# Second ConvFFN of a decoder trunk: eight of its eleven pairs of inner tiles by Strassen's seven products, in four groups instead of two

## The chip, the cores and the metric

The kernel runs on one core of a Trainium2 chip. Its time is the device time of one execution in microseconds (us); lower is better. The profile is one execution recorded by the hardware profiler: PE is the matrix engine (TensorE), PEld its loading of stationary operands, DVE is VectorE, ACT is ScalarE, POOL is GpSimd and SP is SyncE, which here only issues transfers.

## The reference

Two layers on one sequence of 512 tokens and width 1024, all in float32: a Conformer convolution module, a ConvFFN, a retention layer, a second ConvFFN, then a last RMSNorm. The change is in the second ConvFFN, whose inner width F is 2816, that is 22 tiles of 128:

```python
def conv_ffn(x, w_in, dw_w, dw_b, w_out):
    h = x @ w_in                          # 512x1024 @ 1024x5632
    a, u = jnp.split(h, 2, axis=-1)
    a = causal_dwconv(a, dw_w, dw_b)      # three taps along the tokens
    return (jax.nn.silu(a) * u) @ w_out   # 512x2816 @ 2816x1024
...
h = rmsnorm(x, norm_ffn_g[i])
x = x + conv_ffn(h, ffn_w_in[i], ffn_dw_w[i], ffn_dw_b[i], ffn_w_out[i])
...
return rmsnorm(x, final_g)
```

## The kernel before

**Precision.** Each float32 operand is held as a high part (a cast to fp32r) and a low part (the difference). One product of tiles takes three matmuls: high with high, low with high, high with low (`mm3`, lines 309 to 311). Every weight chunk is therefore loaded raw (`wr`, four buffers of 128 x 2048, issued on SP), cast by ACT (`wh`, line 239, four buffers of 128 x 1024) and subtracted by DVE (`wl`, line 243, four buffers). `weights()` hands out the current unit of weights and emits the next one.

**Layout.** The residual x is kept transposed: `xT[k]` holds features 128k to 128k+127 on the partitions and the 512 tokens along the free axis.

**The plain form** (`ffn_half`). For each inner tile f, `mm(f)` computes one 128 x 512 tile of `a` (`fa`) and one of `u` (`fu`): 8 tiles of x times 3 matmuls for each, 48 matmuls of 512 columns. A pair of tiles takes two units of weights (four halves of 128 x 1024). x is taken times the norm's gain only; the factor 1/rms (`rb`, made by `n3.stats` and `n3.bcast` in the course of the first tiles) is applied when the tiles are read out. `evac(f)` does that read-out: `ap` = `fa` x `rb` on DVE, three taps (`taps`: ACT, two on DVE, Silu on ACT), `rb` once more on POOL, times `fu` on DVE, and the split into `y_f` high and low. A generator `each` is advanced after every `evac`; a generator `side` is advanced inside it.

**The block form** (`ffn_blocks`, so far used in the first ConvFFN for 14 of its 22 tiles). A pair of inner tiles is a 2 x 2 block product: x cut in two by features (k below 4, k from 4) and in two by tokens (256 columns each), the weights in two by features and into `a` and `u`. Strassen's scheme (Winograd's variant) needs seven block products instead of eight; each is 2 tiles x 4 x 3 = 24 matmuls of 256 columns. The left factors are the four quarters of the normed x and four sums of them (`Factors`: `sums_of(k)` and `normed_split(k)`). The right factors are made from two raw chunks by `pair_factor`: one sum on DVE (`ws`, line 281), and three sums by transfers that add into the raw tile (lines 282, 292 and 294, issued on POOL). The products accumulate in three pairs of PSUM banks, `z`, `x` and `p`; between products ACT copies out `q1`, `u1` and `u2`.

**After a group of tiles** their `y` tiles are taken times the matching rows of `w_out` (`lo`: for the two halves g of the output columns and four tiles tb of tokens, three matmuls of 512 columns for each inner tile), and `finish` adds the result to x. This projection is token major, so x is transposed before it: DVE transposes in blocks of 32 (line 1287) into `xq`, and 16 transfers on SP for each batch (`quarters`, line 433) put the blocks in place in `xt`. Before, that is done by `token_major`, one transpose per inner tile of the first group, in three batches of 3, 3 and 2 tiles of x. In the last projection `finish` also takes the sum of squares, the last norm and the output transfers (lines 1299 to 1313).

**Groups.** `GROUPS` lists for each ConvFFN the ranges of inner tiles and whether each is done in block form. Before, the second ConvFFN has two plain groups, tiles 0 to 11 and 12 to 21.

**Order.** The tile framework orders every engine's instructions at build time by a simulated timeline. It fills an engine's waits with later work that is ready, so the order on an engine differs in places from the order in the code. At run time each engine goes through its list in order.

Of the kernel before, what the change touches and what calls it, by code (L numbers as in the profile page):

```python
# [9 lines left out]
F32 = mybir.dt.float32  # L10
# [6 lines left out]
P = 128  # L17
D = 1024
S = 512
KD = D // P  # L20
NTB = S // P
# [5 lines left out]
NF = F // P  # L27
EPS = 1e-6

GROUPS = [[(0, 8, False), (8, 14, True), (14, 22, True)], [(0, 12, False), (12, 22, False)]]  # L30

# [21 lines left out]
NSH = 9  # L55
GC = P // PH
NM = NSH * PH * GC
XG = ((0, 3), (3, 3), (6, 2))


COLS = {"mg": 16, "fg": 16, "dwb": 8, "lng": 8, "lnb": 8, "taps": CW * KD, "dwp": PH * len(PHASED), "fw0": 4 * NF, "fw1": 4 * NF}
# [95 lines left out]
def trunk(ctx, tc, xt_d, positions, ret_gn_g, final_g, weights_d, cols_d, mats_d, ident_d, decay_d, invf_d, out):  # L157
    nc = tc.nc
    pe, act, dve, pool = nc.tensor, nc.scalar, nc.vector, nc.gpsimd
# [3 lines left out]
    xp = ctx.enter_context(tc.tile_pool(name="xp", bufs=1))  # L163
# [110 lines left out]
    sum_pool = [None]  # L274
# [70 lines left out]
    xT = [xs_all[:, k, :] for k in range(KD)]  # L345
# [8 lines left out]
    class Rstd:  # L354


        def __init__(self, name):
            self.name = name
# [60 lines left out]
    QB = 32  # L419

    def blocks(t):

        return t.rearrange("p (a b q) -> p a b q", a=NTB, q=QB)
# [5 lines left out]
    def quarters(dst, src, *engs):  # L429

        for p in range(P // QB):
            for c in range(P // QB):
                engs[c % len(engs)].dma_start(dst[c * QB:(c + 1) * QB, :, p, :], src[p * QB:(p + 1) * QB, c, :, :])
# [439 lines left out]
    N2 = S // 2  # L873

    class Factors:
        def __init__(self, norm, xs, pool_, other):
            self.norm, self.xs, self.other = norm, xs, other
            self.sums = [pool_.tile([P, 4, 4, N2], F32R, tag=f"s{half}", bufs=1, name=f"{norm.name}s{half}") for half in "hl"]

        def normed(self, k):  # L880
            n = self.norm
            t = xp.tile([P, S], F32, tag="nsq", bufs=2, name=f"{n.name}n{k}")
            dve.scalar_tensor_tensor(out=t, in0=xT[k], scalar=n.gain[:, k:k + 1], in1=n.rb, op0=ALU.mult, op1=ALU.mult)
            return t

# [27 lines left out]
    def ffn_blocks(fp, l, norm, f0, f1, left, side=None):  # L913

        ys = []
        for f in range(f0, f1, 2):
            def bank(which):
                return [psum(f"f{which}{l}_{f + j}")[:, :N2] for j in range(2)]

            def product(pss, which, first=False):  # L920
                w = weights()
                for j, ps in enumerate(pss):
                    for k, (xh, xl) in enumerate(left.factor(which)):
                        mm3(ps, *w(k, j * P, (j + 1) * P), xh, xl, first and k == 0, k == 3, skip_group_check=not first)

            def kept(pss, name):
                tiles = [fp.tile([P, N2], F32, tag=name, bufs=2, name=f"{name}{l}_{f + j}") for j in range(2)]
                for t, ps in zip(tiles, pss):
                    act.copy(t, ps)
                return tiles  # L930

            lo, hi = slice(0, N2), slice(N2, S)
            aps = [fp.tile([P, S + 32], F32, tag="ap", bufs=2, name=f"ap{l}_{f + j}") for j in range(2)]
            us = [fp.tile([P, S], F32, tag="fy", bufs=2, name=f"fy{l}_{f + j}") for j in range(2)]
            z = bank("z")
            product(z, "x11", True)
            q1 = kept(z, "q1")
            x = bank("x")
            product(x, "x12", True)
            for j in range(2):  # L940
                dve.memset(aps[j][:, :2], 0.0)
                dve.tensor_tensor(out=aps[j][:, 2:2 + N2], in0=x[j], in1=q1[j], op=ALU.add)
            p = bank("p")
            product(p, "s1", True)
            product(z, "s2")
            u1 = kept(z, "u1")
            product(z, "s3")
            u2 = kept(z, "u2")
            for j in range(2):
                dve.tensor_tensor(out=us[j][:, hi], in0=p[j], in1=u2[j], op=ALU.subtract)  # L950
            product(z, "x22")
            ts = []
            for j in range(2):
                act.copy(aps[j][:, 2 + N2:2 + S], z[j])
                ts.append(taps(fp, l, f + j, aps[j]))
            product(p, "s4")
            for j in range(2):
                dve.tensor_tensor(out=us[j][:, lo], in0=p[j], in1=u1[j], op=ALU.subtract)
                dve.tensor_tensor(out=us[j], in0=us[j], in1=ts[j], op=ALU.mult)
                ys.append(split(us[j], f"y{l}_{f + j}", ("yh", "yl"), fp))  # L960
                next(side or iter(()), None)
        return ys
# [55 lines left out]
    with ExitStack() as es:  # L1018
        fp = es.enter_context(tc.tile_pool(name="f0", reuse_waits="tile", bufs=8))
        sum_pool[0] = fp  # L1020
        left = Factors(n1, list(n1.xs), fp, lambda name: fp.tile([P, 2, N2], F32, tag="fy", bufs=2, name=name))
# [250 lines left out]


    with ExitStack() as es:
        fp = es.enter_context(tc.tile_pool(name="f1", reuse_waits="tile", bufs=12))
        lp = es.enter_context(tc.tile_pool(name="lp", reuse_waits="tile", bufs=1))
        xt = lp.tile([P, NTB, 4, KD * QB], F32, name="xt")
        fgb = (cos, sin)
        for g in range(2):
            act.dma_start(fgb[g], final_g[512 * g:512 * (g + 1)].partition_broadcast(P))  # L1280

        def token_major():

            for k0, kn in XG:
                xq = lp.tile([P, 4, NTB, kn, QB], F32, tag="xq", bufs=1, name=f"xq{k0}")
                for k in range(kn):
                    dve.transpose(xq[:, :, :, k, :].rearrange("p c t q -> p t c q"), blocks(xT[k0 + k]))
                    yield
                quarters(xt[:, :, :, k0 * QB:(k0 + kn) * QB], xq.rearrange("p c t k q -> p c t (k q)"), nc.sync)

        ssq = sp.tile([P, NTB, 2], F32, tag="ssq", bufs=1, name="ssq")

        def finish(n, g, tb, ps):
            d = xt[:, tb].rearrange("p a (k q) -> p k a q", q=QB)[:, 4 * g:4 * g + 4]
            if n == 0:
                dve.tensor_tensor(out=d, in0=blocks(ps), in1=d, op=ALU.add)
                return
            dv, d = d, xT[2 * tb + g]
            dve.tensor_tensor(out=blocks(d), in0=blocks(ps), in1=dv, op=ALU.add)
            j = xp.tile([P, S], F32, tag="nsq", bufs=2, name=f"junk{tb}{g}")  # L1300
            v = ssq[:, tb, g:g + 1]
            act.activation(j, d, AF.Square, accum_out=v)
            if g == 0:
                dve.tensor_scalar(out=v, in0=v, scalar1=1.0 / D, scalar2=EPS, op0=ALU.mult, op1=ALU.add)
                pool.tensor_tensor(out=d, in0=d, in1=fgb[0], op=ALU.mult)
                return
            vv = sp.tile([P, 1], F32, tag="fv", name=f"fv{tb}")
            dve.tensor_scalar(out=vv, in0=v, scalar1=1.0 / D, scalar2=ssq[:, tb, 0:1], op0=ALU.mult, op1=ALU.add)
            r = rsqrt_small(vv, 1, f"fr{tb}")
            act.activation(xT[2 * tb], xT[2 * tb], AF.Copy, scale=r)  # L1310
            nc.scalar.dma_start(out[0, tb * P:(tb + 1) * P, :512], xT[2 * tb])
            dve.scalar_tensor_tensor(out=d, in0=d, scalar=r, in1=fgb[1], op0=ALU.mult, op1=ALU.mult)
            nc.sync.dma_start(out[0, tb * P:(tb + 1) * P, 512:], d)

        for n, (f0, f1, _) in enumerate(GROUPS[1]):
            ys = ffn_half(fp, 1, n3, f0, f1, () if n else (None, n3.stats, n3.bcast), None if n else token_major())
            nk = len(ys)
            for g in range(2):
                last = n == 1 and g == 1
                ps = [psum(f"lo{n}{g}{tb}") for tb in range(NTB)]  # L1320
                groups = []
                for k0, kn in _out_chunks(f0, f1, last):
                    groups += [(k0 + k, k, w) for w in [weights()] for k in range(kn)]
                    if last and k0 + kn < nk and k0 > 0:
                        continue
                    for tb in range(NTB):
                        for f, k, w in groups:
                            yh, yl = ys[f]
                            mm3(ps[tb], yh[:, tb * P:(tb + 1) * P], yl[:, tb * P:(tb + 1) * P], *w(k, 0, 512),
                                f == 0, f == nk - 1)  # L1330
                        if k0 + kn == nk:
                            finish(n, g, tb, ps[tb])
                    groups = []
# [79 lines left out]
```

## Time and profile before

| | |
|---|---|
| Time before, median of 3 runs | 1281.57 us (1281.56 to 1282.28) |
| Profiled execution, its own time | 1281.37 us |
| Its span, first to last instruction | 1279.6 us |
| Granted TensorE clock | 0.998 |
| Busy: PE, PEld, DVE, ACT, POOL | 1270.1, 1082.6, 882.9, 566.1, 271.0 us |
| HBM read, written | 133.75 MB, 2.10 MB |

The second ConvFFN runs from 911.80 us (first `fa` matmul) to the end of the span. Busy times are sums of instruction times on an engine; matmuls overlap, so the time that one costs in a stream is the distance between starts, which a window's length over its count of matmuls gives (`x` counts also include an instruction that reaches into the window). A line such as `[0.37 <-PE fa L311]` behind an instruction says how long its engine sat idle before it and what ended that.

### The profile page before, as it was taken

The page shows a single profiled execution, that of the slowest core. Times are in us where ns is not written, and L with a number is a line of the kernel's source. Part 1 is how long each engine was busy: PE and PEld are TensorE (multiplying, and loading weights), DVE is VectorE, ACT ScalarE, POOL GpSimd, SP SyncE. Part 2 cuts the span into 40 slices and gives each one's busy share as a digit, 9 for nine tenths or more (in the row PEclk, how much of TensorE's full clock was granted, in tenths as well). Part 3 has the DMA queues.
Part 4 walks back from the last instruction along what each step waited for, and adds up shares of the span by engine and source line. Part 5 has one row for each costly group of instructions (what it writes and reads, how often), then busy time and mean ns, then how long its engine had stood idle before and what let it go on. Part 6 is the DMA issues. An engine that isn't in the chain of part 4 may idle for free.

```text
span 1279.6 us, 16389 instructions
## 1 busy us (share of the span) xinstructions
PE 1270.1 (99%) x6459; PEld 1082.6 (85%) x6459; DVE 882.9 (69%) x1210; ACT 566.1 (44%) x796; POOL 271.0 (21%) x250
## 2 busy tenths in 40 slices
PE   9999999999999999999999999999999999999997
PEld 7889988888998998888888888878888888888886
DVE  6998658884796897589696686695675642355542
ACT  6546644442652665335344345254443431143332
POOL 0957321110100110222212303203311100011111
PEclk9999999999999999999999999999999999999999
DMA  9533331333755663322405315323124432223111
GB/s 331 229 124 107 126 114 66 127 111 83 190 153 133 184 167 130 115 99 81 126 25 187 109 41 173 82 100 132 66 99 123 124 116 99 99 70 128 34 66 66
DMA packets 38957, 151.58 MB, mean 118 GB/s; under 512 B 11232, under 2 KB 16096, under 8 KB 24800
## 3 DMA queue, kind: packets, MB, share of 16 engines
q1 hardware_dynamic: 32256, 134.02, 30.5%
q0 software_dynamic: 3024, 11.01, 4.7%
q10 hardware_dynamic: 3600, 5.52, 1.5%
q8 instruction: 50, 0.82, 0.3%
q14 instruction: 27, 0.22, 0.1%
HBM read 133.75 MB, written 2.10 MB: 106 GB/s over the span
## 4 chain that ended last, share of the span: by engine, by line
PE 97%; DVE 2%; issue 1%; POOL 0%; ACT 0%; POOLq 0%
PE fu L310 4%; PE fa L310 4%; PE fa L311 4%; PE fu L311 4%; PE fa L309 4%; PE fu L309 4%; PE fo L310 3%; PE fo L309 3%; PE fo L311 3%; PE lo L310 3%; PE lo L311 3%; PE lo L309 3%; PE cph L622 3%; PE qk L309 2%; PE qk L310 2%; PE qk L311 2%
## 5 line engine op out<-in xcount | busy, mean ns | idle before, releaser
L243 DVE TENSOR_TENSOR wl<-wr,wh 128x1024 fp32r<-128x1024 f32 (+2 forms) x256 | 314.9, 1234 | 164.4 <-ACT wh L239 161.8
L239 ACT CAST wh<-wr 128x1024 fp32r<-128x1024 f32 (+2 forms) x258 | 264.9, 1030 | 329.2 <-PE lo L310 63.5
L1107 POOL TENSOR_TENSOR gg<-gg,gn 128x512 f32<-128x512 f32 x16 | 27.5, 1721 | 179.3 <-ACT gg L1106 179.3
L998 POOL MEMSET ap<- 128x2 f32 x30 | 2.8, 98 | 277.8 <-DVE ft L972 239.9
L671 DVE SCALAR_TENSOR_TENSOR tp<-hp,prm,tp 128x512 f32<-128x512 f32 x80 | 55.8, 748 | 0.4
L970 ACT ACTIVATE ft<-ap,prm 128x512 f32<-128x512 f32 x44 | 35.9, 815 | 43.2 <-DVE ap L999 42.7
L662 POOL TENSOR_TENSOR pla<-pla,plt 128x512 f32<-128x512 f32 x36 | 49.1, 1366 | 9.7 <-ACT pla L658 5.6
L1003 DVE TENSOR_TENSOR fy<-fu,ft 128x512 f32<-128x512 f32 x30 | 20.6, 688 | 39.3 <-PE fu L311 23.9
L973 ACT ACTIVATE ft<-ft 128x512 f32<-128x512 f32 x44 | 27.7, 632 | 37.2 <-DVE ft L972 36.5
L971 DVE SCALAR_TENSOR_TENSOR ft<-ap,prm,ft 128x512 f32<-128x512 f32 x44 | 33.9, 771 | 11.6 <-ACT ft L970 11.4
L1091 POOL TENSOR_TENSOR rs<-rs 128x512 f32<-128x512 f32 x16 | 24.7, 1559 | 67.4 <-DVE rs L1090 42.3
L1001 POOL TENSOR_TENSOR ft<-ft,n3r 128x512 f32<-128x512 f32 x22 | 32.2, 1464 | 28.7 <-ACT ft L973 28.7
L661 ACT ACTIVATE plt<-hp,prm 128x512 f32<-128x512 f32 x36 | 25.8, 722 | 20.7 <-POOL pla L662 20.2
L972 DVE SCALAR_TENSOR_TENSOR ft<-ap,prm,ft 128x512 f32<-128x512 f32 x44 | 33.9, 771 | 0.8
L467 DVE TENSOR_TENSOR xT<-ro,xT 128x512 f32<-128x512 f32 x32 | 21.6, 682 | 16.5 <-PE ro L311 16.5
L622 PEld LDWEIGHTS cph<-ph,cmat 128*128 128x128 f32 x288 | 32.6, 192 | 0.2
L622 PE MATMUL cph<-ph,cmat 128*128 128x128 f32 x288 | 32.6, 275 | 0.0
L311 PE MATMUL fp<-n1sl,wh 128*128 128x256 f32 x112 | 31.7, 283 | 0.0
L310 PE MATMUL fp<-n1sh,wl 128*128 128x256 f32 x112 | 31.7, 283 | 0.0
L309 PE MATMUL fp<-n1sh,wh 128*128 128x256 f32 x112 | 31.7, 283 | 0.0
L311 PE MATMUL fz<-n1sl,wh 128*128 128x256 f32 x112 | 31.6, 283 | 0.0
L310 PE MATMUL fz<-n1sh,wl 128*128 128x256 f32 x112 | 31.6, 283 | 0.0
(1969 smaller groups left out, 4010.2 us busy)
## 6 DMA issues: line engine op xcount, KB each, us to landing
wr<-in_weights_dram SPq DMA_DIRECT2D x106, 1024.0 KB, 5.0
cmat<-in_mats_dram SPq DMA_DIRECT2D x4, 2304.0 KB, 11.2
wr<-wr POOLq DMA_DIRECT2D x14, 512.0 KB, 4.5
wr<-in_weights_dram POOLq DMA_DIRECT2D x7, 512.0 KB, 5.9
wr<-in_weights_dram SPq DMA_DIRECT2D x4, 512.0 KB, 3.6
wr<-in_weights_dram SPq DMA_DIRECT2D x6, 256.0 KB, 7.7
yt<-yq ACTq DMA_DIRECT2D x24, 64.0 KB, 2.1
yt<-yq SPq DMA_DIRECT2D x24, 64.0 KB, 2.1
```

The source lines that it names most:

```text
L239: latest[0] = act.copy(hi[:, o:o + n], raw[:, s + o:s + o + n])
L243: latest[1] = low_on.get(i, dve).tensor_tensor(out=lo[:, o:o + n], in0=raw[:, s + o:s + o + n], in1=hi[:, o:o + n].bitcast(F32), op=ALU.su ...
L309: pe.matmul(ps, wh, xh, start=first, stop=False, **check)
L310: pe.matmul(ps, wl, xh, start=False, stop=False, **check)
L311: pe.matmul(ps, wh, xl, start=False, stop=last, **check)
L622: pe.matmul(ps[:, g * P:(g + 1) * P], mats[i][g][:, s, :], ph[:, g, NSH - 1 - s:NSH - 1 - s + P], start=s == 0, stop=s == NSH - 1)
L662: gate[0] = pool.tensor_tensor(out=pl, in0=pl, in1=tm, op=ALU.add).ins
L671: dve.scalar_tensor_tensor(out=a, in0=hp[:, t:t + S], scalar=tap(t, i), in1=a, op0=ALU.mult, op1=ALU.add)
L970: act.activation(t, ap[:, 2:2 + S], AF.Identity, scale=wc(2), bias=wc(3))
L971: dve.scalar_tensor_tensor(out=t, in0=ap[:, 1:1 + S], scalar=wc(1), in1=t, op0=ALU.mult, op1=ALU.add)
L972: dve.scalar_tensor_tensor(out=t, in0=ap[:, 0:S], scalar=wc(0), in1=t, op0=ALU.mult, op1=ALU.add)
L1001: scaled = pool.tensor_tensor(out=t, in0=t, in1=norm.rb, op=ALU.mult)
```

## The change

The second ConvFFN gets four groups: tiles 0 to 5 plain, and 6 to 11, 12 to 17 and 18 to 21 in block form, 8 pairs in all. Around it:

- x is transposed at once (8 transposes, then one batch of 16 transfers) in the generator `between`, which runs between the plain tiles; it goes on to make the sums and the quarters for the left factors. The buffer `xq` shares its place (`sh`) with the high parts of the sums.
- `normed(k)` writes x times gain and `rb` in place into `xT[k]`, once, and keeps it.
- `q1`, `u1` and `u2` of the second ConvFFN live in the buffers of the norms (`nacc`, `nsq`).
- `finish` adds to x after each of the first three groups. The last projection has 4 inner tiles, so it has one chunk of weights for each half g.

```diff
-GROUPS = [[(0, 8, False), (8, 14, True), (14, 22, True)], [(0, 12, False), (12, 22, False)]]
+GROUPS = [[(0, 8, False), (8, 14, True), (14, 22, True)], [(0, 6, False), (6, 12, True), (12, 18, True), (18, 22, True)]]
...
-        def __init__(self, norm, xs, pool_, other):
-            self.norm, self.xs, self.other = norm, xs, other
+        def __init__(self, norm, xs, pool_, other, in_place=False):
+            self.norm, self.xs, self.other, self.made = norm, xs, other, {} if in_place else None
...
         def normed(self, k):
             n = self.norm
-            t = xp.tile([P, S], F32, tag="nsq", bufs=2, name=f"{n.name}n{k}")
+            if self.made and k in self.made:
+                return self.made[k]
+            if self.made is None:
+                t = xp.tile([P, S], F32, tag="nsq", bufs=2, name=f"{n.name}n{k}")
+            else:
+                t = self.made[k] = xT[k]
             dve.scalar_tensor_tensor(out=t, in0=xT[k], scalar=n.gain[:, k:k + 1], in1=n.rb, op0=ALU.mult, op1=ALU.mult)
             return t
...
             def kept(pss, name):
-                tiles = [fp.tile([P, N2], F32, tag=name, bufs=2, name=f"{name}{l}_{f + j}") for j in range(2)]
+                if l == 0:
+                    tiles = [fp.tile([P, N2], F32, tag=name, bufs=2, name=f"{name}{l}_{f + j}") for j in range(2)]
+                else:
+                    home, n = ("nacc", 1) if name == "q1" else ("nsq", 2)
+                    t = xp.tile([P, 2, N2], F32, tag=home, bufs=n, name=f"{name}{l}_{f}")
+                    tiles = [t[:, 0], t[:, 1]]
...
-        fp = es.enter_context(tc.tile_pool(name="f1", reuse_waits="tile", bufs=12))
+        fp = es.enter_context(tc.tile_pool(name="f1", reuse_waits="tile", bufs=6))
...
+        sum_pool[0] = fp
...
-        def token_major():
-
-            for k0, kn in XG:
-                xq = lp.tile([P, 4, NTB, kn, QB], F32, tag="xq", bufs=1, name=f"xq{k0}")
-                for k in range(kn):
-                    dve.transpose(xq[:, :, :, k, :].rearrange("p c t q -> p t c q"), blocks(xT[k0 + k]))
+        lefts = []
+
+        def between():
+            xq = fp.tile([P, 4, NTB, KD, QB], F32, tag="sh", bufs=1, name="xq")
+            for k in range(KD):
+                dve.transpose(xq[:, :, :, k, :].rearrange("p c t q -> p t c q"), blocks(xT[k]))
+            yield
+            quarters(xt, xq.rearrange("p c t k q -> p c t (k q)"), nc.sync)
+            left = Factors(n3, list(n3.xs), fp, lambda name: fp.tile([P, 2, N2], F32, tag="fy", bufs=2, name=name), True)
+            lefts.append(left)
+            for k in range(4):
+                left.sums_of(k)
+                if k < 3:
                     yield
-                quarters(xt[:, :, :, k0 * QB:(k0 + kn) * QB], xq.rearrange("p c t k q -> p c t (k q)"), nc.sync)
+            for k in range(KD):
+                left.normed_split(k)
...
-            if n == 0:
+            if n < len(GROUPS[1]) - 1:
                 dve.tensor_tensor(out=d, in0=blocks(ps), in1=d, op=ALU.add)
...
-        for n, (f0, f1, _) in enumerate(GROUPS[1]):
-            ys = ffn_half(fp, 1, n3, f0, f1, () if n else (None, n3.stats, n3.bcast), None if n else token_major())
+        for n, (f0, f1, by_blocks) in enumerate(GROUPS[1]):
+            if by_blocks:
+                ys = ffn_blocks(fp, 1, n3, f0, f1, lefts[0])
+            else:
+                side = between()
+                ys = ffn_half(fp, 1, n3, f0, f1, (None, n3.stats, n3.bcast), each=side)
+                for _ in side:
+                    pass
             nk = len(ys)
             for g in range(2):
-                last = n == 1 and g == 1
+                last = n == len(GROUPS[1]) - 1 and g == 1
```

More of the change, by code (lines that the diff above doesn't have):

```diff
@@ L57 @@
 NM = NSH * PH * GC
-XG = ((0, 3), (3, 3), (6, 2))
 COLS = {"mg": 16, "fg": 16, "dwb": 8, "lng": 8, "lnb": 8, "taps": CW * KD, "dwp": PH * len(PHASED), "fw0": 4 * NF, "fw1": 4 * NF}
```

## The prediction

> **What bounds the kernel now.** I read the page's head, the chain that ended last and the PE's waits first.
>
> ```profile
> span 1279.6 us, 16389 instructions
> ...
> PEclk9999999999999999999999999999999999999999
> ...
> PE 97%; DVE 2%; issue 1%; POOL 0%; ACT 0%; POOLq 0%
> ```
>
> ```profile
> PE warm L179 <- POOL ones L324: 1.0, 1, 1.0
> PE vg3z L311 <- DVE wl L243: 0.5, 1, 0.5
> PE vg3p L311 <- DVE wl L243: 0.5, 1, 0.5
> ```
>
> PE carries 97% of the chain and waits 2.0 us in all, none of it in a ConvFFN; its clock is granted in full throughout. So in the second ConvFFN a microsecond of matmul issue saved is a microsecond of time, as long as every other engine stays ahead. What a matmul costs there, and in the block form, is read from windows: two plain pairs of the second ConvFFN; two block pairs of the first; half of a projection; then the second ConvFFN's first six tiles, the first ConvFFN's plain group, and its last block group.
>
> ```profile
> core 0: us, PE busy (x) PEld busy (x) DVE busy (x) ACT busy (x) POOL busy (x), PEclk, DMA share, GB/s
> 1109.11:1152.63 43.52, 43.52 (x194) 36.05 (x192) 23.80 (x28) 15.85 (x19) 5.31 (x8) 1.00 0.25 85
> 412.84:453.16 40.32, 40.32 (x338) 40.32 (x337) 33.08 (x50) 25.31 (x39) 5.24 (x6) 1.00 0.62 164
> 1043.83:1109.11 65.28, 65.28 (x290) 54.07 (x288) 19.64 (x21) 13.30 (x14) 0.98 (x1) 1.00 0.30 105
> 911.80:977.10 65.30, 65.30 (x289) 53.59 (x288) 42.90 (x51) 27.51 (x36) 11.53 (x13) 1.00 0.28 91
> 190.10:270.40 80.30, 80.30 (x355) 66.12 (x355) 62.86 (x93) 36.69 (x49) 11.30 (x14) 1.00 0.26 89
> 407.10:491.00 83.90, 83.90 (x688) 83.31 (x687) 71.10 (x107) 51.99 (x81) 7.05 (x9) 1.00 0.64 170
> ```
>
> Plain: 2 x 96 = 192 matmuls of 512 columns in 43.52 us, 226.7 ns each, 21.76 us a pair. Block: 2 x 168 = 336 of 256 columns in 40.32 us, 120.0 ns each, 20.16 us a pair. Half the columns cost 53% of the time; in the block window PEld is busy throughout, in the plain one for 83%. So seven eighths of the arithmetic is worth 7.4%, not 12.5%.
>
> **Part by part.**
>
> *The products.* 8 pairs x (21.76 - 20.16) = **-12.80 us** on PE. The projection keeps its 528 matmuls (22 tiles x 24) at 226.7 ns (288 in 65.28 us), whatever the groups: 0.
>
> *The weights.* A plain pair needs four casts and four low parts, a block pair seven of each, one sum on DVE and three adding transfers on POOL.
>
> ```profile
> L243 DVE TENSOR_TENSOR wl<-wr,wh 128x1024 fp32r<-128x1024 f32 (+2 forms) x256 | 314.9, 1234 | 164.4 <-ACT wh L239 161.8
> L239 ACT CAST wh<-wr 128x1024 fp32r<-128x1024 f32 (+2 forms) x258 | 264.9, 1030 | 329.2 <-PE lo L310 63.5
> ...
> wr<-wr POOLq DMA_DIRECT2D x14, 512.0 KB, 4.5
> wr<-in_weights_dram POOLq DMA_DIRECT2D x7, 512.0 KB, 5.9
> ```
>
> Added: ACT 24 x 1.03 = 24.7 us, DVE 24 x 1.23 and 8 sums priced alike = 39.5 us, 24 transfers. All of it lies beside PE: the last block group of the first ConvFFN has DVE busy for 71.10 of 83.90 us (85%) and PE never waits there, with the rotary tables on DVE besides, which the second ConvFFN does not have. Cost 0. If the cover went, PE would pay for the late factor of each product.
>
> *Read-out.* The block form drops POOL's product with `rb` and adds copies of 256 columns on ACT and subtractions on DVE; they are in the windows just used. The four groups add 16 `finish` sums on DVE, about 0.7 us each (11 us over the 260 us or so before the last projection), in the projections, where DVE is busy for 19.64 of 65.28 us: 0.
>
> *Preparation of the left factors.* It must fit beside six plain tiles (65 us) and their projection (6 x 24 x 0.2267 = 32.6 us). DVE was busy for 42.90 of the 65.30 us there. Against the first ConvFFN: that one puts its sums into a plain group of eight tiles, DVE 62.86 of 80.30 us, without a wait of PE. In place, eight of its sixteen `normed` products go; the eight transposes come together.
>
> ```profile
> L1287 DVE STREAM_TRANSPOSE xq<-xT x8: 700/702/712, 947.8 to 1023.7; 128x512 f32<-128x512 f32 x8
> ```
>
> ```profile
> 969.32 10.33 SPq L433 DMA_DIRECT2D xt<-xq  x16
> 979.75 18.04 SPq L212 DMA_DIRECT2D wr<-in_weights_dram  x3
> 1002.66 11.19 SPq L433 DMA_DIRECT2D xt<-xq  x16
> ...
> 1024.42 10.25 SPq L433 DMA_DIRECT2D xt<-xq  x16
> ```
>
> ```profile
> SPq L212 <- DVE wl L243: 789.1, 91, 34.4
> ```
>
> ```profile
> 1015.53 0.71 DVE L1287 STREAM_TRANSPOSE xq<-xT 128x512 f32<-128x512 f32 x1 [2.01 <-DMA xt<-xq]
> ```
>
> Transposes: 8 x 0.70 = 5.6 us of DVE. Transfers: one batch (about 10.3 us of SP's queue) for three (31.8 us), each transfer larger (2 MB / 16 = 128 KB). SP stands idle for a free buffer for 789 us in all, so weight loads behind the batch have room. New is a wait: the sums' first high part on ACT needs the buffer of `xq`, so it waits for the sixteenth transfer. The same kind of wait held DVE for 2.01 us before. Behind it on ACT stand the weight casts, and behind those PE. Their room:
>
> ```profile
> 948.87 1.05 ACT L239 CAST wh<-wr 128x1024 fp32r<-128x1024 f32 x1 [0.37 <-PE fa L311]
> ...
> 949.96 1.23 DVE L243 TENSOR_TENSOR wl<-wr,wh 128x1024 fp32r<-128x1024 f32 x1 [0.73 <-ACT wh L239]
> ...
> 956.79 0.39 PE L309 MATMUL fa<-n3x0h,wh 128*128 128x512 f32 x1
> ```
>
> The low part is done at 951.2 and used from 956.8: 5.6 us. A wait of 2 us disappears in that; one of all 10 us would cost 10.3 - 5.6 = 4.7 us, once. I take 0, since the nearest row is the 2.01; bounds 0 and +4.7. A gain is excluded, as PE has no wait there to lose.
>
> *From the last pair into the last projection.* New: the last group has four tiles, so the projection needs y_20 and y_21 almost at once; before, ten tiles gave cover. Nearest is the first ConvFFN's last pair, whose last product starts its last matmul at 490.83:
>
> ```profile
> 490.83 0.28 PE L311 MATMUL fp<-n1sl,wh 128*128 128x256 f32 x1
> ...
> 495.43 0.68 DVE L386 TENSOR_TENSOR y_20l<-fy,y_20h 128x512 fp32r<-128x512 f32 x1
> 496.04 0.42 DVE L512 TENSOR_SCALAR rot<-rot 128x512 f32<-128x512 f32 x1
> 496.37 0.68 DVE L386 TENSOR_TENSOR y_21l<-fy,y_21h 128x512 fp32r<-128x512 f32 x1
> ```
>
> y_21's low part is there at 497.05, 6.1 us after the product; about 2.2 us of that is rotary work, so 3.9 us here. PE can cover 5.4 us with y_18 and y_19 on all four token tiles (24 matmuls x 0.2267), if the build-time order has not spent them earlier. Bounds: 0, and 6.1 less the 2.5 us before y_21's low part comes up in code order, +3.6. I take **+0.7**, near the lower end, because in the first ConvFFN that order puts projection work (`fo`) ahead of the last pair's product x22 (`fz`), where PE would else have waited:
>
> ```profile
> 481.99 1.09 PE L309 MATMUL fo<-y_14h,wh 128*128 128x512 f32 x4
> 482.92 0.28 PE L309 MATMUL fz<-n1n4h,wh 128*128 128x256 f32 x1
> ```
>
> *The tail.* Each token tile's last `finish` now follows after 12 matmuls (2.72 us) instead of 24 (5.44).
>
> ```profile
> 1272.51 0.69 DVE L1299 TENSOR_TENSOR xT<-lo,xt 128x512 f32<-128x512 f32 x1 [2.34 <-PE lo L311]
> ...
> 1274.28 0.54 POOL L351 TENSOR_TENSOR fr3y<-fv,minus_half 128x1 f32<-128x1 f32 x1 [4.90 <-DVE fv L1308]
> ...
> 1274.85 0.75 DVE L1312 SCALAR_TENSOR_TENSOR xT<-xT,fr3y,sin 128x512 f32<-128x512 f32 x1 [0.66 <-POOL fr3y L351]
> ```
>
> From the sum to the last product on DVE it is 3.09 us, more than 2.72: if the next tile's sum stands behind this tile's last product, each is 0.37 us later than the one before, three times: +1.1. Interleaved it is 0. I take **+0.7**; no gain, since the chain after the last matmul is unchanged.
>
> **Sum:** -12.80 + 0.7 + 0.7 = -11.4 us. The profiled execution took 1281.37 us, 0.2 below the median of 1281.57; from the median the change gives 1270.2, and I say **1270.1 us**.
>
> **The rivals.**
>
> *Preparation crowds PE.* The wait for `xq`'s transfers is longer than ACT's room, or evac of tile 5 stands behind the eight splits and comes late. For it: DVE would be near full there (42.90 + 5.6 + the sums, of 65.30 us). Against it: the first ConvFFN did nearly as much without a wait. Price: up to 4.7 us for the wait and, if y_5 is as late as y_21 can be, up to 3.6 us for that: 2 to 8 us on top, 1272 to 1278.
>
> *A matmul of 256 columns at half the price of one of 512.* Then a block pair would take 168 x 113.3 = 19.04 us, the products would bring 8 x 2.72 = 21.8 us, and the time would be 1261. The block window speaks against it with 120.0 ns over 336 matmuls; only a different stationary operand could change that, and the products are the same. The Trainium skill, "TensorE: Matmul & The Clock Gate", section "Back-to-back issue gap", gives the isolated gap as columns over 2.4 GHz plus 2.5 ns, and adds that with weight loads between them small matmuls fall behind that. By its figures the estimate is 215.8 and 109.2 ns, a saving of 19.0 us over the eight pairs, 1264. The windows, 226.7 and 120.0, decide.
>
> *Slower: the adding transfers come late.* Place: the low half of the weights for the product x22 waits for a transfer that adds into its raw tile.
>
> ```profile
> 474.63 1.05 ACT L239 CAST wh<-wr 128x1024 fp32r<-128x1024 f32 x1 [1.49 <-DMA wr<-wr]
> ...
> 476.33 2.47 DVE L243 TENSOR_TENSOR wl<-wr,wh 128x1024 fp32r<-128x1024 f32 x2
> ```
>
> In the first ConvFFN ACT did wait 1.49 us for one, and DVE had that factor ready at 477.5; the product began only at 482.9, so 5.4 us were left. A transfer that took 4.5 + 5.4 us would begin to hold PE, and every further microsecond costs 8. The sum is used up at 11.4 / 8 = 1.4 us a pair, so it turns slower once landing takes about 11.3 us on every pair, against 4.5 (and 5.9 from HBM). At 2 us a pair: 1286. The load on the queues is that of the first ConvFFN, which speaks against it. The Trainium skill, "SBUF — State Buffer", section "SBUF: two separate sides", warns that a transfer issued from GpSimd can be kept waiting for its descriptors while VectorE runs a two-port operation. No run here shows that by itself; the 4.5 us were measured with DVE busy.
>
> **How the numbers follow.** The forecast, with PE losing under 3 us, 1268.4 to 1272.0: 0.78. Preparation: 0.13. Half price: 0.01. Late transfers: 0.08, of which 0.03 end within 0.2% (2.6 us, about what a measurement of this kernel can tell from no change) of the time before. So faster 0.92, same 0.03, slower 0.05. The range starts at -12.8 (1268.8, less 0.4 for scatter) and reaches 1274.5: all upper bounds of the last two terms (-12.8 + 3.6 + 1.1 = -8.1, 1273.5) and 1 us of preparation.
>
> **What the profile after would show.** Block pairs of 20.16 us in the second ConvFFN, 168 starts 120 ns apart; PE waits still near 2 us in all. ACT idle before the first high part of the sums, released by the transfers of `xq`, under 5.6 us. A PE gap, if any, where the last pair hands over to `lo`, under 1 us. The last four sums on DVE 2.7 to 3.1 us apart. The prediction fails if starts of 256-column matmuls are not 120 ns apart, if PE waits on `wl` in block pairs, or if the plain group of six takes well over 65.3 us.

## The result, and the profile after

| | before | after |
|---|---|---|
| Median of the runs, us | 1281.92 (1281.56 to 1282.29) | 1270.35 (1269.84 to 1270.83) |
| Profiled execution: its own time, us | 1281.37 | 1270.41 |
| Its span, us | 1279.6 | 1268.6 |
| Instructions | 16389 | 17818 |

The ratio is 0.9911, 95% interval 0.9899 to 0.9923. The change makes the kernel faster by 11.6 us (medians); the two profiled executions differ by 11.0 us. The forecast was 1270.1 us.

The page's head after, its clock row and the chain that ended last:

```profile
span 1268.6 us, 17818 instructions
...
PEclk9999999999999999999999999999999999999999
...
PE 95%; DVE 3%; issue 1%; POOL 1%; DMA 0%; ACT 0%; SPq 0%; POOLq 0%; DVEq 0%
```

PE still sets the time, at full clock. DVE has one percent more of the chain. That percent does not come from the tail: by the same chain in order of time it lies from 898.47 us to 917.2 us, a run of DVE work with six of the eight transposes in it, and it ends at PE's new wait. POOL's percent lies in the tail. The waits of PE after:

```profile
...
PE fu L309 <- DVE wl L242: 0.2, 1, 0.2
```

The three rows left out are those of before; this fourth one is new. It lies in the first plain tile, not in the blocks. The windows after are those of two block pairs, of two more, of the six plain tiles, and of the first projection behind them; the columns are as in the prediction.

```profile
1013.00:1053.30 40.30, 40.30 (x338) 40.30 (x337) 28.05 (x39) 24.15 (x38) 4.35 (x5) 1.00 0.59 155
1106.20:1146.50 40.30, 40.30 (x338) 40.30 (x337) 28.05 (x39) 24.15 (x38) 4.41 (x5) 1.00 0.61 156
912.10:979.28 67.18, 66.94 (x296) 54.75 (x294) 58.04 (x88) 34.24 (x48) 12.81 (x12) 1.00 0.35 99
979.28:1011.92 32.64, 32.64 (x146) 27.03 (x144) 21.40 (x26) 9.13 (x13) 5.94 (x5) 1.00 0.59 171
```

Two block pairs hold 336 starts in 40.30 us: 119.9 ns each, 20.15 us a pair. The six plain tiles take 67.18 us, of which PE works all but 0.24, with DVE at 86%.

To see where the 11 us came from, I cut the span at four matmuls. First before (first `fa`, the first matmul after six plain tiles, the last matmul), then after (the first `fa`, the first matmul of the first projection, the seam between the last product and the last projection, the last matmul), each from PE's timeline:

```profile
911.80 0.39 PE L309 MATMUL fa<-n3x0h,wh 128*128 128x512 f32 x1
...
978.55 0.39 PE L309 MATMUL fa<-n3x0h,wh 128*128 128x512 f32 x1
...
1272.08 0.39 PE L311 MATMUL lo<-wl,y_21h 128*128 128x512 f32 x1
```

```profile
912.10 0.39 PE L308 MATMUL fa<-n3x0h,wh 128*128 128x512 f32 x1
...
917.26 0.50 PE L309 MATMUL fu<-n3x0h,wl 128*128 128x512 f32 x1 [0.23 <-DVE wl L242]
...
979.28 0.39 PE L308 MATMUL lo<-wh,y_0h 128*128 128x512 f32 x1
...
1240.58 0.28 PE L310 MATMUL fp<-n3sl,wh 128*128 128x256 f32 x1
1240.69 0.40 PE L308 MATMUL lo<-wh,y_19h 128*128 128x512 f32 x1
...
1260.25 0.39 PE L310 MATMUL lo<-wl,y_21h 128*128 128x512 f32 x1
```

| stretch | before, us | after, us | difference |
|---|---|---|---|
| to the first `fa` (not changed) | 911.80 | 912.10 | +0.30 |
| six plain tiles | 66.75 | 67.18 | +0.43 |
| from there to the end of the last matmul | 293.92 | 281.36 | -12.56 |
| from there to the start of DVE's last product | 2.38 | 3.23 | +0.85 |
| sum | | | -10.98 |

The first row is scatter: when the changed kernel was run again (the last comparison below), its first `fa` began at 911.62, ahead of both. The third row is the products' -12.80 and +0.24 that was not traced further.

### The profile page after: what moved, and what is told of

Read it like the earlier page. It is cut to its first block, busy times and chain, and to the rows that moved or that the text cites. A ratio compares the mean times of both kernels' runs of the same rounds, so it can differ in the third digit from the quotient of the medians.

```text
span 1268.6 us, 17818 instructions
## 1 busy us (share of the span) xinstructions
PE 1257.9 (99%) x7035; PEld 1099.1 (87%) x7035; DVE 949.8 (75%) x1346; ACT 617.5 (49%) x900; POOL 269.0 (21%) x242
## 4 chain that ended last, share of the span: by engine, by line
PE 95%; DVE 3%; issue 1%; POOL 1%; DMA 0%; ACT 0%; SPq 0%; POOLq 0%; DVEq 0%
PE fz L310 5%; PE fz L309 5%; PE fz L308 5%; PE fo L308 3%; PE fo L309 3%; PE fo L310 3%; PE lo L308 3%; PE lo L309 3%; PE lo L310 3%; PE cph L621 3%; PE qk L308 2%; PE qk L309 2%; PE qk L310 2%; PE fp L309 2%; PE fp L308 2%; PE fp L310 2%
## 5 line engine op out<-in xcount | busy, mean ns | idle before, releaser
L242 DVE TENSOR_TENSOR wl<-wr,wh 128x1024 fp32r<-128x1024 f32 (+2 forms) x272 | 334.0, 1233 | 143.5 <-ACT wh L238 140.8
L238 ACT CAST wh<-wr 128x1024 fp32r<-128x1024 f32 (+2 forms) x274 | 281.7, 1032 | 284.5 <-PE lo L309 49.3
L938 ACT COPY u<-fz 128x256 f32<-128x256 f32 x60 | 22.4, 373 | 35.4 <-PE fz L310 33.7
L281 POOL DMA_DIRECT2D wr<-in_weights_dram x15 | 13.5, 898 | 113.2 <-DVE ws L280 61.4
L309 PE MATMUL fp<-n3sh,wl 128*128 128x256 f32 x128 | 36.2, 283 | 0.0
L308 PE MATMUL fp<-n3sh,wh 128*128 128x256 f32 x128 | 36.2, 283 | 0.0
L310 PE MATMUL fp<-n3sl,wh 128*128 128x256 f32 x128 | 36.2, 283 | 0.0
L309 PE MATMUL fz<-n3sh,wl 128*128 128x256 f32 x128 | 36.1, 283 | 0.0
L310 PE MATMUL fz<-n3sl,wh 128*128 128x256 f32 x128 | 36.1, 283 | 0.0
L308 PE MATMUL fz<-n3sh,wh 128*128 128x256 f32 x128 | 35.9, 283 | 0.0
```

The lines of the kernel that those rows point to most:

```text
L238: latest[0] = act.copy(hi[:, o:o + n], raw[:, s + o:s + o + n])
L242: latest[1] = low_on.get(i, dve).tensor_tensor(out=lo[:, o:o + n], in0=raw[:, s + o:s + o + n], in1=hi[:, o:o + n].bitcast(F32), op=ALU.su ...
L308: pe.matmul(ps, wh, xh, start=first, stop=False, **check)
L309: pe.matmul(ps, wl, xh, start=False, stop=False, **check)
L310: pe.matmul(ps, wh, xl, start=False, stop=last, **check)
```

## The experiments

The theory (A): PE issues without a pause in the second ConvFFN, so the time moves by the number of matmuls times the distance between their starts, 120.0 ns at 256 columns and 226.7 at 512, and nothing else in the change matters by more than a microsecond. Its rivals: a block pair is held by something other than PE's issue (its weights, its read-out, its adding transfers); 256 columns are cheap or dear because of something else than their number; the small losses come from the preparation's wait for `xq`.

**One product more: eight instead of seven.** `x12` of the second ConvFFN is computed twice.

```diff
-for k, (xh, xl) in enumerate(left.factor(which)):
-    mm3(...)
+for _ in range(2 if l == 1 and which == "x12" else 1):
+    for k, (xh, xl) in enumerate(left.factor(which)):
+        mm3(...)
```

> Adds an eighth product to each of the eight block pairs of the second ConvFFN (the product x12 is computed twice, the second time over the first). Theory A (matmul issue alone is the bound in block pairs, 120.0 ns a matmul): 24 x 0.120 = 2.88 us a pair, 23.0 us in all, so 1270.4 + 23.0 = 1293.4 us, slower than the kernel before by 0.9%, and block pairs of 23.04 us. Theory B (PE's lead over DVE and ACT is thin, so that part of an added product only fills time in which PE would wait for factors): the pairs would grow by less, and the time would stay under 1288.

Measured: 1293.7 us (1293.35 to 1293.95), ratio 1.0093 (1.0076 to 1.011). Against the changed kernel's 1270.35 that is +23.35, where 8 pairs x 24 x 0.120 = 23.04. Two pairs in its windows:

```profile
1013.00:1059.10 46.10, 46.10 (x387) 46.10 (x386) 28.37 (x40) 24.18 (x38) 4.34 (x5) 1.00 0.54 137
```

384 starts in 46.10 us, 120.1 ns. The weights and the read-out are the same, DVE and ACT have the same work, and the pair is longer by the whole product. Nothing in the block pairs was slack that a product could fill: PE's issue is the bound. This also gives the price of the block form without Strassen's saving: slower than before by 0.93%, though the arithmetic is equal.

**One product fewer.** The matmuls of `s4` are left out, so this kernel does six products of the seven.

```diff
 w = weights()
+if l == 1 and which == "s4":
+    return
```

> Leaves out the product s4 in the eight block pairs of the second ConvFFN (its weights are still made; the first half of u lacks that term). Theory A: 24 matmuls fewer a pair, 17.28 us, the time falls by 23.0 us to 1247.3, as DVE (28.05 of 40.30 us in two pairs, 14.0 a pair) and ACT (24.15, 12.1 a pair) still fit. Theory B: the factors, the copies between products and the read-out then end last; the pairs stay above 18 us and the time above 1253.

Measured: 1249.68 us (1248.54 to 1250.27), ratio 0.9749 (0.9735 to 0.9764); 20.7 us below the changed kernel instead of 23.0. The window of two pairs, PE's waits, and DVE's end:

```profile
1013.00:1047.60 34.60, 34.60 (x291) 34.60 (x290) 27.14 (x38) 22.81 (x36) 3.51 (x4) 1.00 0.69 175
```

```profile
PE fz L308 <- ACT u L940: 0.4, 1, 0.4
```

```profile
1243.66 0.75 DVE L1333 SCALAR_TENSOR_TENSOR xT<-xT,fr3y,sin 128x512 f32<-128x512 f32 x1 [0.66 <-POOL fr3y L350]
```

The pairs themselves are right: 17.30 us each, 288 starts at 120.1 ns. Some 2.4 us did not come. Its trace shows 0.4 us of a wait for ACT's copy, once, between two products of the third block pair (at 1059.32), 1.5 us in the tail (its last matmul ends at 1238.91, so the tail is 4.75 us against 3.23), and a start of the second ConvFFN that was 0.75 us later, in a part that was not edited. So seven of the eight pairs have cover for a product less (2.88 us a pair), and the chains around PE begin to show, in the tail first.

**One group less in block form.** Tiles 12 to 17 are plain again, fed with the quarters already normed (their `rb` is a tile of ones), so five block pairs.

```diff
-(0, 6, False), (6, 12, True), (12, 18, True), (18, 22, True)
+(0, 6, False), (6, 12, True), (12, 18, False), (18, 22, True)
```

> The same four groups, but the third (tiles 12 to 17) in the plain form on the normed quarters: five block pairs instead of eight. Theory A (the gain is 1.60 us a block pair, whatever the groups): 3 x 1.60 = 4.8 us back, 1275.2 us. Rival (the gain comes with the groups and the relief of POOL and DVE around them, not from the number of matmuls): less than 2 us back, below 1272.5.

Measured: 1275.22 us (1274.99 to 1275.43), ratio 0.9949 (0.9935 to 0.9964): +4.87 against the changed kernel, where 3 x 1.60 = 4.80. Its three plain pairs:

```profile
1105.10:1170.40 65.30, 65.30 (x290) 54.09 (x289) 34.94 (x43) 23.98 (x29) 8.33 (x10) 1.00 0.22 74
```

288 starts in 65.30 us, 226.7 ns. So a pair is worth 1.6 us, with five pairs done as with eight.

**The price of a matmul by its columns.** A stretch of bare matmuls ahead of the second ConvFFN, 32 of each shape: 128, 192, 256, 320, 384 and 512 columns with a stationary operand of 128 x 128, then 256 and 512 columns with one of 64 columns.

```diff
+for c, m in ((128, P), (192, P), (256, P), (320, P), (384, P), (512, P), (256, 64), (512, 64)):
+    ps = psum(f"bench{c}_{m}")
+    with pe_in_order():
+        for r in range(4):
+            for k in range(KD):
+                pe.matmul(ps[:m, :c], n3.xs[k][0][:, r * P:r * P + m], n3.xs[(k + 1) % KD][0][:, :c], ...)
```

> Ahead of the second ConvFFN, 32 matmuls each with 128, 192, 256, 320, 384 and 512 columns and a stationary operand of 128 x 128, then 256 and 512 columns with a stationary operand of 128 x 64; all in fp32r, results unused. Theory L (up to 256 columns the load of the stationary operand sets the distance between starts): 128, 192 and 256 columns all near 112 to 120 ns, 384 and 512 on the line of the moving columns (170 and 226.7), and with the narrower stationary operand 256 columns fall to about 113 ns. Theory F (a fixed 13.3 ns and 0.4168 ns a column, the line through 120.0 and 226.7): 66.7, 93.4, 120.0, 146.7, 173.4, 226.7 ns, and no change with 64 columns of stationary operand.

It was executed once, and only its trace is read. The windows of it that lie at full clock: 128 columns, 256, 320, 384, 512, and 256 with the narrow stationary operand. They run from one start to another; `x` also counts instructions that reach in.

```profile
917.36:918.02 0.66, 0.66 (x7) 0.66 (x8) 0.66 (x2) 0.30 (x1) 0.00 (x0) 1.00 0.00 0
929.02:932.38 3.36, 3.36 (x31) 3.36 (x29) 0.00 (x0) 0.00 (x0) 0.00 (x0) 1.00 1.00 202
932.50:937.05 4.55, 4.55 (x34) 4.55 (x32) 0.00 (x0) 0.00 (x0) 0.00 (x0) 1.00 0.36 77
937.20:942.57 5.37, 5.37 (x33) 5.37 (x32) 0.00 (x0) 0.00 (x0) 0.00 (x0) 1.00 0.00 0
943.90:949.81 5.91, 5.91 (x27) 4.88 (x26) 0.00 (x0) 0.00 (x0) 0.00 (x0) 1.00 0.01 3
950.16:953.56 3.40, 3.40 (x33) 3.40 (x31) 0.00 (x0) 0.00 (x0) 0.00 (x0) 1.00 0.00 0
```

| columns | starts apart in the window | ns each | 13.3 + 0.417 x columns |
|---|---|---|---|
| 128 | 6 in 0.66 us | 110 | 66.7 |
| 256 | 28 in 3.36 | 120.0 | 120.0 |
| 320 | 31 in 4.55 | 146.8 | 146.7 |
| 384 | 31 in 5.37 | 173.2 | 173.4 |
| 512 | 26 in 5.91 | 227.3 | 226.7 |
| 256, stationary 64 wide | 30 in 3.40 | 113.3 | |
| 512, stationary 64 wide | 30 in 6.90 (from 953.90) | 230.0 | |

The times that theory L named came out within some 3 ns at full clock. Theory F fails twice: at 128 columns (110 ns, not 66.7) and with the narrow operand at 256 columns (113.3, where it allowed no change). Still, from 256 columns up with the full operand F's line holds, the one through the kernel's two prices: 0.417 ns a column and 13.3 ns for each matmul. Below it there is a floor of some 110 ns. It is the same for 128 and 192 columns: where both ran at half clock, starts were 214 ns apart at 128 columns (16 in 3.42 us from 918.35) and 213 at 192 (27 in 5.76 us from 922.25). That the floor is the load of the stationary operand, which is L's reason, fits the narrow operand, which takes 6.7 ns off at 256 columns and nothing at 512, but it was not isolated. For this change it matters that 256 columns lie on the line: with it, the 13.3 ns are why seven eighths of the arithmetic gave 7.4%.

**The transposes behind the norm.** The eight transposes of x are held until `n3.diag`, a late step of the norm's statistics, so the build-time order cannot draw them forward among the low parts of the first plain tile.

```diff
-dve.transpose(xq[...], blocks(xT[k]))
+with tc.issue_after(n3.diag):
+    dve.transpose(xq[...], blocks(xT[k]))
```

> The eight transposes are ordered behind the diagonal of n3 on DVE, so they run after the norm's statistics instead of between the end of the retention and the first plain tiles. Theory A (the transposes drawn forward delayed the low part that the first u tile waits for, 0.4 us of PE): PE no longer waits on wl before the first fu tile, the six plain tiles take 66.75 us as before instead of 67.18, and the time falls by 0.4 us to about 1270.0. Rival (the shared buffer of xq is the cost, and it only stayed hidden because the transfers were early): the transfers end about 13 us later, ACT then waits for them with the weight casts behind it, and the plain tiles take 1 to 5 us longer, 1271.5 to 1275.

First what there is to mend, in the changed kernel: DVE's timeline ahead of the 0.23 us wait, and the tiles `xq` and `n3sh`.

```profile
914.52 0.70 DVE L1298 STREAM_TRANSPOSE xq<-xT 128x512 f32<-128x512 f32 x1
...
915.72 1.48 DVE L242 TENSOR_TENSOR wl<-wr,wh 128x1024 fp32r<-128x1024 f32 x1
```

```profile
L432 SPq DMA_DIRECT2D xt<-xq x16: 585/600/1144, 919.7 to 931.6; - x16
L1298 DVE STREAM_TRANSPOSE xq<-xT x8: 693/696/711, 899.3 to 918.9; 128x512 f32<-128x512 f32 x8
...
DMA to landing us min/median/max: 2.8/5.9/7.1
```

```profile
L902 ACT CAST n3sh<-n3sa x4: 606/614/621, 943.6 to 969.9; 128x512 fp32r<-128x512 f32 x4
```

The transposes run from 899.3 us on, so from before the first `fa`; one of them stands ahead of the low part that PE waits for. The transfers are issued by 931.6 and land within 7.1 us, and ACT's first high part of the sums comes at 943.6: neither ACT nor PE waits for `xq`. (DVE once sat idle for 1.1 us until one of these transfers, by the same view, at 928.0 us; PE did not wait for that low part.) Held back:

```profile
L432 SPq DMA_DIRECT2D xt<-xq x16: 594/602/642, 932.1 to 941.9; - x16
L1299 DVE STREAM_TRANSPOSE xq<-xT x8: 667/668/703, 927.2 to 931.4; 128x512 f32<-128x512 f32 x8
```

Measured: 1270.43 us (1270.13 to 1270.8), ratio 0.991 (0.9895 to 0.9925); by the times alone, nothing. In its trace PE's fourth wait is gone, and from the first matmul on `yt30`, in the retention layer's output projection, to the first `lo` it takes 88.67 us, against 89.08 in the changed kernel; before, to the first matmul after six plain tiles, it took 88.64. So the 0.4 us came back in its place. In the two traces a later start of that stretch (891.00 against 890.20 us, scatter again) hides it.

**The last group of six tiles.** The groups are 0 to 5, 6 to 9, 10 to 15 and 16 to 21, so the last projection has 18 matmuls for each token tile instead of 12.

```diff
-(0, 6, False), (6, 12, True), (12, 18, True), (18, 22, True)
+(0, 6, False), (6, 10, True), (10, 16, True), (16, 22, True)
```

> Groups of 6 plain, then 4, 6 and 6 tiles in block form, so that the last projection has six inner tiles and two chunks of weights. Theory A (the tail is 0.85 us longer because the finish of the token tiles crowds into the last projection of four tiles, with 2.72 us of matmuls each): the time from the last matmul's end to the last product on DVE goes from 3.23 back towards the 2.38 us of before, the time falls by 0.5 to 0.9 us to about 1269.7. Rival (the tail is set by how PE's order interleaves the two halves g, not by the number of tiles): the tail stays at 3.2 us and the time at 1270.4.

Measured: 1270.14 us (1269.99 to 1270.41), ratio 0.9909 (0.9895 to 0.9922). DVE's end in the changed kernel, then here:

```profile
1260.35 0.74 DVE L1331 SCALAR_TENSOR_TENSOR xT<-xT,fr1y,sin 128x512 f32<-128x512 f32 x1
1261.01 0.68 DVE L1318 TENSOR_TENSOR xT<-lo,xt 128x512 f32<-128x512 f32 x1
1261.61 0.74 DVE L1331 SCALAR_TENSOR_TENSOR xT<-xT,fr2y,sin 128x512 f32<-128x512 f32 x1
...
1263.87 0.75 DVE L1331 SCALAR_TENSOR_TENSOR xT<-xT,fr3y,sin 128x512 f32<-128x512 f32 x1 [0.66 <-POOL fr3y L350]
```

```profile
1260.57 0.75 DVE L1331 SCALAR_TENSOR_TENSOR xT<-xT,fr2y,sin 128x512 f32<-128x512 f32 x1 [0.65 <-POOL fr2y L350]
1261.24 0.69 DVE L1318 TENSOR_TENSOR xT<-lo,xt 128x512 f32<-128x512 f32 x1
...
1263.58 0.75 DVE L1331 SCALAR_TENSOR_TENSOR xT<-xT,fr3y,sin 128x512 f32<-128x512 f32 x1 [0.66 <-POOL fr3y L350]
```

The last matmul ends at 1260.64 in the changed kernel and at 1260.90 here. In the first the last sum begins 0.37 us after it, behind a product of tile 1; the product of tile 2 comes after it. Here tile 2's product is ahead of it and the sum begins 0.34 after the matmul, but the chain behind runs free: 2.68 us to the last product against 3.23. So the tail pays 0.55 us for a last group of four inner tiles. What crowds it is POOL, which in `finish` takes the four tiles of the first half of the columns times the last norm's gain. First the changed kernel, then this one:

```profile
1254.05 5.05 POOL L1324 TENSOR_TENSOR xT<-xT,cos 128x512 f32<-128x512 f32 x4 [33.98 <-ACT junk L1321]
1259.07 0.57 POOL L350 TENSOR_TENSOR fr0y<-fv,minus_half 128x1 f32<-128x1 f32 x1
```

```profile
1243.43 5.05 POOL L1324 TENSOR_TENSOR xT<-xT,cos 128x512 f32<-128x512 f32 x4 [34.98 <-ACT junk L1321]
```

In the changed kernel these four stand on POOL ahead of the 1/rms of token tile 0 (`fr0y`), whose input was ready at 1257.41, so it comes some 1.6 us late, and the last products of tiles 0, 1 and 2 crowd in beside the last sum. Here they are done by 1248.48. (The groups before the last were moved as well; the trace shows no wait of PE from that.)

**Both edits together**, once by themselves and once more beside an unedited changed kernel on the same chip:

> Both edits, the transposes behind the norm's diagonal and the last projection with six tiles. Theory A: the two losses are at different places and add, 0.4 + 0.5 to 0.9: about 1269.3 us. Rival (either of them fails as above): 1270.4 or more.

> The changed kernel as it is, beside the next three. Every theory: 1270.35 us within 0.5.

> The kernel of e7 (transposes behind the norm's diagonal, last projection of six tiles) beside the changed kernel on one chip. Theory A: shorter than the changed kernel by what the two traces show at the two places, 0.41 us in the first tiles and 0.55 us in the tail, 0.96 us together: 1269.4. Rival (1269.62 against 1270.35 was scatter between chips): the two within 0.3 us of each other.

Measured: 1269.62 us (1269.39 to 1269.95), ratio 0.9904 (0.9891 to 0.9918). In the second comparison 1269.70 (1269.07 to 1270.11), ratio 0.9905 (0.9891 to 0.9919), beside the changed kernel's 1270.48 (1269.99 to 1270.78), ratio 0.9911 (0.9898 to 0.9925). The medians differ by 0.78 us where 0.96 was expected, and the ranges overlap by 0.12 us; the ratios' intervals do not tell the two apart. In the two traces the tails are 2.67 and 3.22 us, and that stretch to the first `lo` 88.66 and 89.13. Of the versions that leave nothing out it is the fastest that was run.

**Transposed at once, without the blocks.** The kernel before, its two plain groups kept, with the change's transposes: eight, then one batch of transfers. For room, `ft` has two buffers instead of three.

```diff
-for k0, kn in XG:
-    xq = lp.tile([P, 4, NTB, kn, QB], ...)
-    for k in range(kn):
-        dve.transpose(xq[...], blocks(xT[k0 + k]))
-        yield
-    quarters(xt[...], ...)
+xq = lp.tile([P, 4, NTB, KD, QB], ...)
+for k in range(KD):
+    dve.transpose(xq[...], blocks(xT[k]))
+yield
+quarters(xt, ...)
```

> The kernel before with one part of the change alone: x transposed at once and one batch of 16 transfers, both groups still plain (ft has two buffers instead of three, for room). Theory A (the products alone bring the gain; the transposes cost the 0.4 us seen in the changed kernel's first tiles or nothing): 1281.9 to 1282.4. Rival (part of the 11.6 us comes from the transposes and the two batches of transfers saved): 1279 or less.

Measured: 1284.99 us (1283.69 to 1285.76), ratio 1.0022 (1.0013 to 1.0031). It was expected to do nothing and costs 3.1 us. DVE's timeline, PE's waits, and PE in the stretch of the wait and behind it:

```profile
914.97 3.08 DVE L1286 STREAM_TRANSPOSE xq<-xT 128x512 f32<-128x512 f32 x5
917.97 1.18 DVE L243 TENSOR_TENSOR wl<-wr,wh 128x1024 fp32r<-128x1024 f32 x1
```

```profile
PE fu L310 <- DVE wl L243: 1.8, 1, 1.8
```

```profile
917.00:919.20 2.20, 0.41 (x2) 0.00 (x0) 2.20 (x4) 0.00 (x0) 0.00 (x0) 1.00 0.00 0
919.20:922.70 3.50, 3.49 (x10) 2.73 (x11) 3.50 (x6) 0.00 (x0) 0.00 (x0) 0.60 0.08 18
```

Five transposes stand in a row ahead of the low part of `fu`'s first weights. PE waits 1.80 us for it. Then its clock falls: in the next 3.50 us about 10 matmuls start where 15.4 would at 226.7 ns, another 1.2 us. Together 3.0, about the loss. The eleven times lie in two clusters, five from 1283.69 to 1284.23 us and six from 1284.99 up; the trace is of one in the upper cluster. That the lower one is the wait without the fall of the clock would fit, but no trace shows it.

**The same, behind the norm.** The one line of the experiment above, `with tc.issue_after(n3.diag):`, on top of this one.

> The kernel of e8 (the kernel before with x transposed at once) with the transposes ordered behind the norm's diagonal. Theory A (e8 lost 3.1 us because five transposes stood on DVE ahead of the low part that the first u tile waits for, and the clock fell to half after that wait): the wait is gone, 1281.9 us within 0.4. Rival (the one large batch of transfers, or the two buffers of ft, cost it): 1284 to 1285.5.

Measured: 1281.75 us (1281.44 to 1282.73), ratio 0.9999 (0.999 to 1.0008). So it was the transposes' place on DVE, not their number, the single batch or the buffers of `ft`; and transposing at once brings nothing by itself.

**Not in place.** `Factors` makes its sixteen products anew, eight more on DVE.

```diff
-left = Factors(n3, ..., True)
+left = Factors(n3, ..., False)
```

> The changed kernel with the normed x made twice into separate buffers instead of once in place: 8 more products of 0.67 us on DVE, 5.4 us, in the first projection, where DVE is busy for 21.40 of 32.64 us. Theory A (all of it lies beside PE): 1270.4 within 0.5. Rival (DVE is short of time there, y_5 or the quarters for the first block pair come late): 1 to 4 us longer, 1271.4 to 1274.5.

Measured: 1270.65 us (1270.36 to 1271.15), ratio 0.9914 (0.9901 to 0.9928). In the first projection DVE is busy for 27.80 instead of 21.40 us, and PE issues its 144 starts in the same time:

```profile
979.30:1012.00 32.70, 32.70 (x146) 27.09 (x145) 27.80 (x36) 11.30 (x16) 5.14 (x5) 1.00 0.56 165
```

The in-place edit saves 6.4 us of DVE there, all of it beside PE.

## Why the prediction was right, step by step

- *Products, -12.80.* Right, and the cause is shown: block pairs of 20.15 us, one product more or one fewer moves a pair by 24 matmuls of 120 ns, and three pairs fewer cost 3 x 1.6 us.
- *Weights, read-out, projection, 0.* Right. No row of PE's waits names `wl`, `wh` or a copy in a block pair, with DVE busy for 28.05 of 40.30 us there. The rival of late adding transfers did not happen: they took 4.6 us in the median, as in the first ConvFFN.

```profile
wr<-wr POOLq DMA_DIRECT2D x30, 512.0 KB, 4.6
```

- *Preparation, 0 (bounds 0 and +4.7).* The sum was nearly right, the mechanism was not. The wait that was priced, ACT's for `xq`'s transfers, did not occur: the first high part came some 5 us after the last landing. What cost 0.43 us was a step not priced at all: the transposes need nothing of the norm, so the build-time order drew them ahead of the first tiles' low parts on DVE. The prediction had counted their 5.6 us but not asked whom they would stand in front of. The experiment on the kernel before shows what it can cost, 3.1 us, where the range's upper end had allowed 1 us for the preparation. That it was 0.43 here and not more is luck: nothing in the prediction bounded this wait.
- *The six plain tiles "well over 65.3 us".* That criterion was set on a wrong base: the window of 65.30 us is 288 matmuls, and the same six tiles took 66.75 us before, as this stretch also holds other matmuls. By the right base it is +0.43.
- *Hand-over from the last pair, +0.7.* Too much; it was 0. The product `fp` ends its issue at 1240.58 and `lo` goes on at 1240.69, with y_19. DVE's timeline:

```profile
1246.30 0.69 DVE L385 TENSOR_TENSOR y_21l<-fy,y_21h 128x512 fp32r<-128x512 f32 x1 [0.69 <-ACT y_21h L384]
```

  y_21's low part is there at 1246.99, 6.4 us after the product began its last matmul and not the 3.9 that were estimated (here DVE waits for ACT, where in the first ConvFFN it had rotary work; besides, the three rotary rows between 490.83 and 497.05 there add up to 1.5 us, not 2.2). PE never notices: it had y_18 and y_19 for both halves of the output columns, twice the cover that was counted for one. Two errors of opposite sign. The cover has its price, though: with both halves mixed, the first half's sums begin only at 1252.52 us, and this is what puts POOL's four products so late.
- *Tail, +0.7.* Measured +0.85: the size was near, the mechanism mostly another. The last four sums were to stand 2.7 to 3.1 us apart, each a little later than the one before. They began at 1255.46, 1256.60, 1257.96 and 1261.01, as PE's order mixes the token tiles, so nothing added up from tile to tile. The named step is seen once: the last sum begins 0.37 us after the last matmul, behind another tile's product, where it was 0.04 before. The other 0.52 us are ACT's:

```profile
1261.04 1.15 ACTq L1330 DMA_DIRECT2D out_dram<-xT  x2
1262.24 0.63 ACT L1321 ACTIVATE junk<-xT 128x512 f32<-128x512 f32 x1 [0.62 <-DVE xT L1318]
```

  The last square is put down to the sum, but the sum was done at 1261.69. What ends just before the square, at 1262.19, is ACT's issue of the output transfers of tiles 1 and 2. Both losses come from products that POOL's late 1/rms pushed to the end. With a last group of six tiles 0.55 us of the 0.85 goes.
- *Half price for 256 columns* is refuted in the changed kernel's windows, and by the bare matmuls at 120.0 ns.

The trace's terms are -12.56, +0.43 and +0.85, with +0.30 of scatter ahead of the change. The sum predicted was -11.4, and they add up to -11.28. So the forecast was right mainly because the one large term was read from a window of the same work. That the errors of the small ones (+0.43 missed, 0.7 too much) cancel is luck.

## What to carry to other kernels

Price a Strassen step by the distance between starts of the smaller matmuls, read from a window, and not by arithmetic: here 7/8 of the products were worth 7.4%. A second level that halves the columns again would lose: by an estimate from the bare matmuls, each matmul of 256 columns at 120 ns would become 7/4 matmuls of 128 at 110 ns, 192 ns. It was not run. Work that becomes ready early (a transpose that needs no statistics) is drawn forward by a build-time order and can stand ahead of what the bounding engine waits for; hold it behind something, and see on that engine's timeline what it displaces. When the last projection is made shorter, read its finish chain on every engine, also on one that is idle most of the time: here POOL's four products held the last tiles' 1/rms, and a last group of six tiles instead of four moved them out of the way.

## What the runs showed of the hardware that was not expected

A pause of PE of about 2 us was followed by several microseconds at a lower granted clock. In the at-once kernel it was the wait of 1.80 us, then 0.60 over 3.5 us. Among the bare matmuls it was two waits of 1.43 and 2.04 us close together; after them the matmuls of 192 columns ran at half clock:

```profile
914.83 0.33 PE L1340 MATMUL bench<-n3x6h,n3x5h 128*128 128x128 f32 x1 [1.43 <-ACT n3x6h L387]
...
917.19 0.33 PE L1340 MATMUL bench<-n3x7h,n3x6h 128*128 128x128 f32 x1 [2.04 <-ACT n3x7h L387]
```

```profile
921.98:928.22 6.24, 6.24 (x30) 6.24 (x31) 0.00 (x0) 0.00 (x0) 0.00 (x0) 0.50 1.07 265
```

The Trainium skill, "TensorE: Matmul & The Clock Gate", section "HAM oscillation — how this bites in real kernels", gives the rule that PE should not idle for more than about 3.4 us at a time. Here the fall followed a single wait of 1.80 us, so the measurement decides: in that trace the wait cost 1.7 times its length (1.80 and then 1.2 us).

And 128 columns cost 110 ns, only 10 less than 256; 192 columns cost the same as 128 where both ran at half clock.
